# Summing modulation vectors over partition blocks on VectorE instead of TensorE, and writing gates as rows when they are computed

## The chip, the cores and the metric

The kernel runs on one core of one Trainium2 chip. The metric is the device time of one execution in microseconds. A core has TensorE (PE in the profile; the loads of its stationary operand are PEld), VectorE (DVE), ScalarE (ACT), GpSimd (POOL) and SyncE (SP), which works through its instructions in order and here issues most loads. ScalarE issues a few DMAs as well.

## The reference

Two layers of a diffusion backbone over 512 latent tokens of width 1024, with 256 context tokens. Each layer is a half-step SwiGLU, a token mixer (windowed attention in layer 0, a Fourier mix in layer 1), and a second half-step SwiGLU. Every sublayer is modulated by vectors that come from a conditioning vector:

```
mod = (silu(c) @ mod_w[i] + mod_b[i]).reshape(-1, 9, 1024)
h   = x * (1 + mod[:, 3j+1]) + mod[:, 3j]                        # shift and scale, sublayer j
y   = 0.5 * (a * silu(g)) @ wo        with a, g = split(h @ wi)  # the half-step SwiGLU
x   = layer_norm(alpha * x + mod[:, 3j+2] * y, g, b)             # gate
```

For layer 0 the vectors are also needed for the context stream, with its own conditioning vector c_ctx. All is float32.

## The kernel before, in words

**Stages.** One after the other: a head that computes the first shift and scale and the first seven weight blocks' products (h0), the rest of the latent half-step FFN of layer 0, the context half-step FFN, attention, then the FFN l1 (second of layer 0), the FFN l2 (first of layer 1), the Fourier mix, and the FFN l3 (second of layer 1). In an FFN the up products (tiles `up`) run over 22 pairs of weight blocks, and the down products (tiles `y`) over 22 blocks of 128 rows.

**Products in three parts.** Every float32 operand is split in a high and a low part (`wh` by ScalarE, `wl` by VectorE, line 177), and a product is three matmuls (line 181). `weights` (line 211) emits the split of a weight three blocks ahead of its use (`SPLIT_AHEAD`), and its load further ahead. A weight block of the down products may first be multiplied by a gate's row (`gate_next`, line 203: `wr<-wr,gr`), so that the gate costs nothing later.

**Modulation.** A vector of 1024 values needs all of a [1024, 1024] matrix. VectorE sums it: `mod_steps` (line 257) works through jobs, each 128 rows of mod_w, and adds row times silu(c) into an accumulator of [128, 1024], `acc`; eight jobs make a vector. Jobs of the vectors 2, 3 and 4 of layer 0 feed two accumulators (latent and context stream), the others one. The jobs are spread over the pairs of up products: 40 in the first FFN, 24 in the context FFN, 40 in l1, 40 in l2, none in l3. The sum over the 128 partitions then follows: `mod_fold` (line 233) transposes blocks of 32x32 on VectorE (`mt`) and reduces them to `mr` [128, 32], which leaves four partial sums in four blocks of 32 partitions. Three jobs later (`MOD_LAG`), `mod_reduce` (line 245) has TensorE add the four blocks with a matrix of ones at the right places (`folder`) into a PSUM bank `mp`, and VectorE adds the bias `mod_b` and writes the vector as columns [128, 8] into `mod`, in four instructions of 32x8.

**Gates.** A gate is needed as a row repeated on all partitions. `gate_row` (line 315), called in `late` (line 686) two pairs before the end of the up products, has ScalarE scale the columns (`gs`), write them to DRAM (`there`, 1024 elements of 4 bytes out of place), and load them back as a row for each partition (`gr`); both DMAs are issued by ScalarE, and the second waits for the first.

**Order.** TensorE's and GpSimd's instructions stay in program order. VectorE's and ScalarE's do so only in marked stretches (`pin`); in the FFNs, where the modulation runs, their order is set by a scheduler at build time from its own estimates. Tiles of [128, 1024] share 42 buffers (`slot`), small ones 20 (`small`). PSUM has two rings of four banks; a pair of up products takes one of each, `mp` took the next in turn.

Of the kernel before, what the change touches and what calls it, by code (L numbers as in the profile page):

```python
# [10 lines left out]
F32 = mybir.dt.float32  # L11
F32R = mybir.dt.float32r
AF = mybir.ActivationFunctionType
ALU = mybir.AluOpType

P = 128
D = 1024
KC = D // P
# [32 lines left out]
P_WIDTH = 648  # L51
CORE_FETCH = 6
CORE_TILES = 5
MOD_LAG = 3
MOD_EARLY = 1
TURN_ACT = 4
BETWEEN = 5
Q_TURN = 3
# [53 lines left out]
class Emitter:  # L112
# [34 lines left out]
    def small(self, shape, nm="sm"):  # L147
        return self.pool.tile(shape, F32, tag="small", name=self.name(nm), bufs=20)

    def hbuf(self, shape, nm):  # L150
        return self.pool.tile(shape, F32R, tag="h", name=self.name(nm), bufs=2)

# [72 lines left out]
    def mod_plan(self, jobs):  # L225
        self.jobs = [(l, v, streams, k) for (l, v, streams) in jobs for k in range(KC)]
        self.mraw = {}
        self.n_mraw = 0
        self.n_job = 0
        self.acc = {}  # L230
        self.due = []

    def mod_fold(self, l, v, s, a):


        nc = self.nc
        turned = self.slot([P, 1024], F32, "mt")
        nc.vector.transpose(turned, a)
        t = self.small([P, D // BLK], "mr")
        nc.vector.tensor_reduce(  # L240
            out=t, in_=turned.rearrange("p (c k) -> p c k", k=BLK), axis=mybir.AxisListType.X, op=ALU.add
        )
        return l, v, s, t

    def mod_reduce(self, l, v, s, t):
        nc = self.nc
        ps = self.bank(nm="mp")
        self.mm(ps[:, : D // BLK], self.folder, t, start=True, stop=True)
        per = P // BLK
        for q in range(per):  # L250
            rows = slice(q * BLK, (q + 1) * BLK)
            cols = slice(v * KC, (v + 1) * KC)
            nc.vector.tensor_tensor(
                self.mod[l][s][rows, cols], ps[rows, q : D // BLK : per], self.mod_b[l][rows, cols], ALU.add
            )

    def mod_steps(self, n, ahead=2):
        nc = self.nc
        for _ in range(n):
            if self.n_job >= len(self.jobs):  # L260
                break
            while self.n_mraw < min(self.n_job + ahead + 1, len(self.jobs)):
                l, v, _, k = self.jobs[self.n_mraw]
                r = self.slot([P, 1024], F32, "mr")
                nc.sync.dma_start(r, self.ins["mod_w"][l, v, k])
                self.mraw[self.n_mraw] = r
                self.n_mraw += 1
            l, v, streams, k = self.jobs[self.n_job]
            r = self.mraw.pop(self.n_job)
            self.n_job += 1  # L270
            while self.due and self.due[0][0] <= self.n_job:
                self.mod_reduce(*self.due.pop(0)[1])
            for s in streams:
                sc = self.silu_c[:, s, k : k + 1]
                if k == 0:
                    a = self.slot([P, 1024], F32, "acc")
                    self.acc[s] = a
                    nc.vector.tensor_scalar(a, r, sc, None, ALU.mult)
                else:
                    a = self.acc[s]  # L280
                    nc.vector.scalar_tensor_tensor(a, r, sc, a, ALU.mult, ALU.add)
                if k == KC - 1:
                    self.due.append((self.n_job + MOD_LAG, self.mod_fold(l, v, s, self.acc.pop(s))))

    def mod_finish(self, upto):
        if upto > self.n_job:
            self.mod_steps(upto - self.n_job)
        while self.due:
            self.mod_reduce(*self.due.pop(0)[1])

    def col(self, l, s, v):
        return self.mod[l][s][:, v * KC : (v + 1) * KC]
# [19 lines left out]
        return G, B  # L312


    def gate_row(self, l, s, j, scale):

        act = self.nc.scalar
        cols = self.small([P, KC], "gs")
        act.activation(cols, self.col(l, s, 3 * j + 2), AF.Copy, scale=scale)
        there = self.dram.tile([KC, P], F32, tag="gate", name=self.name("there"), bufs=2)  # L320
        act.dma_start(there.rearrange("c p -> p c"), cols)
        row = self.slot([P, 1024], F32, "gr")
        act.dma_start(row, there.rearrange("c p -> (c p)").unsqueeze(0).broadcast_to([P, D]))
        return row

    def fold(self, row, w0, n):
# [353 lines left out]
    def half_step(self, ups, down, h, x, N, l, s, j, nxt, quota, first=None, halves=False, held=None, mid=None, out_h=None, keep=True, fold=True, more=None, reach=REACH):  # L680

        us = []
        stat = self.halves_of(us, N)
        st = {}

        def late():
            self.mod_finish(self.n_job)
            gate = self.gate_row(l, s, j, 0.5)
            if fold:
                self.fold(gate, down, NF)  # L690
            else:
                st["gate"] = gate
            if more is not None:
                self.fold(self.gate_row(*more[0], 1.0), more[1], KC)
            stat(0)

        if N == CTX:
            mid = self.ffn_up_rows(ups, h, quota, us, first, late)
        else:
            self.ffn_up(ups, h, N, quota, us, first=first, halves=halves, late=late, held=held)  # L700
        st["x"] = x() if callable(x) else x

        st["ln"] = (l, j)

        def middle():
            if mid is not None:
                mid()
            if keep and nxt is None:
                st["rows"] = self.ln_rows(l, j)

        st["affine"] = None if nxt is None else self.affine_ln(l, j, nxt[0], s, nxt[1])
        if nxt is not None:
            st["h"] = out_h() if out_h is not None else self.new_h("h")
        rest = self.project(down, NF, stat, st, N // P, mid=middle, keep=keep, reach=reach)
        return rest, st


    def head(self):
# [11 lines left out]
        def load(k):  # L730
            raws[k] = []
            for i in range(2):
                r = self.slot([P, 4, 256], F32, "m0")
                sync.dma_start(r, ins["mod_head"][k, i])
                raws[k].append(r)
            if k == 0:
                sync.dma_start(self.mod_b[0], ins["mod_b"][0])
            if k % 2 == 0:
                xts[k // 2] = self.slot([P, 2, SEQ], F32, "xt")
            if k < 2:  # L740
                sync.dma_start(xts[0][:, k], ins["xT"][0][:, k])
            elif k % 2 == 0:
                sync.dma_start(xts[k // 2], ins["xT"][k // 2])
            ws[k] = self.slot([P, HEAD * P], F32, "wr")
            cuts = (0, HEAD_CUT, HEAD * P) if k == 0 else (0, HEAD * P)
            for c0, c1 in zip(cuts, cuts[1:]):
                sync.dma_start(ws[k][:, c0:c1], ins["wi_head"][k][:, c0:c1])
# [106 lines left out]
        load(1)  # L854
        load(2)
        gather(0, 0, KC)
        nc.vector.tensor_copy(bias[:, 0], self.mod_b[0][:, :KC])
        nc.vector.tensor_scalar(bias[:, 1], self.mod_b[0][:, KC : 2 * KC], 1.0, None, ALU.add)
        w_parts(0)
        for _ in whole_chunks(0):  # L860
            pass
# [30 lines left out]
    def constants(self):  # L892
# [3 lines left out]
        nc.vector.memset(self.ones, 1.0)  # L896
        self.mhalf = self.const([P, 16], F32, "mhalf")
        nc.vector.memset(self.mhalf, -0.5)
        self.mod_b, self.mod = [], []
        for l in range(DEPTH):  # L900
            self.mod_b.append(self.const([P, 9 * KC], F32, f"mod_b{l}"))
            self.mod.append([self.const([P, 9 * KC], F32, f"mod{l}_{s}") for s in range(2 if l == 0 else 1)])


# [1 line left out]
    def run(self):  # L906
# [43 lines left out]

        h, held = self.head()
        sync.dma_start(self.ident, ins["ident"])
        sync.dma_start(self.mod_b[1], ins["mod_b"][1])
        self.folder = self.const([P, P], F32, "folder")
        sync.dma_start(self.folder, ins["folder"])
        self.ln_g = self.const([P, 6 * KC], F32, "ln_g")
        self.ln_b = self.const([P, 6 * KC], F32, "ln_b")
        sync.dma_start(self.ln_g, ins["ln_g_col"])
# [53 lines left out]
            w_c0[0], w_c0[1], ch, load_cx, CTX, 0, 1, 0, (0, 1), 3 * KC, first=rest, out_h=ctx_h, keep=False, fold=False  # L1012
        )

        self.fold(self.gate_row(0, 0, 1, 1.0), w_ao, KC)
        stat = self.attention(w_kv, w_q, w_ao, h1, st["h"], rest)
        st = dict(x=x)
        st["affine"] = self.affine_ln(0, 1, 0, 0, 2)
# [48 lines left out]
    def attention(self, w_kv, w_q, w_ao, h1, ch, rest):  # L1067
# [135 lines left out]
        q10 = q_post(1, 0, ps)  # L1203
        mask = self.slot([P, 896], F32, "mask")
        sync.dma_start(mask, ins["mask"])
        nsink = self.const([P, HEADS], F32, "nsink")
        nc.vector.tensor_scalar(nsink, self.sink, -1.0, None, ALU.mult)


        oT = []  # L1210
# [282 lines left out]
def _constants():  # L1493
# [38 lines left out]
    for i, tab in enumerate(dft(SEQ)):  # L1532
# [1 line left out]
    t2 = t2.reshape(2, 2, 2, P, 512).transpose(0, 1, 3, 2, 4)  # L1534
    return {
        "ident": np.eye(P, dtype=np.float32),
        "folder": np.tile(np.eye(BLK, dtype=np.float32), (P // BLK, P // BLK)),
        "mask": mask,
        "rope": rope,
        "dft1": t1.reshape(P, 1024).astype(np.float32),  # L1540
# [4 lines left out]
def _layout(inp):  # L1545
    f = {k: np.asarray(v) for k, v in inp.items()}

    def cols(a):
        n = a.shape[0]
        return a.reshape(n, -1, P).transpose(0, 2, 1)  # L1550
# [9 lines left out]
    m["mod_w"] = f["mod_w"].reshape(DEPTH, KC, P, 9, D).transpose(0, 3, 1, 2, 4)  # L1560
    head = m["mod_w"][0, :2].reshape(2, KC, P, KC, P)
    m["mod_head"] = head.transpose(3, 2, 1, 0, 4).reshape(KC, P, 2, 4, 256).transpose(0, 2, 1, 3, 4)
    m["mod_b"] = cols(f["mod_b"])
    g = f["ln_g"].reshape(6, D)
    b = f["ln_b"].reshape(6, D)
    m["ln_g_col"] = g.reshape(6, KC, P).transpose(2, 0, 1).reshape(P, 6 * KC)
# [39 lines left out]
```

## Time and profile before

| | us |
|---|---|
| the runs shown | 1977.49, 1979.6, 1979.67 |
| their median | 1979.6 |
| the profiled execution | 1976.75 |
| its span | 1974.9 |

The span runs from the first to the last instruction in the trace; the execution's own time is 1.85 us more. The granted TensorE clock was 0.999 of full speed. Times within the trace are counted from the span's start. The names on both sides of `<-` are the program's tiles, written and read; `x` with a number counts instructions. L79 stands for nearly all instructions, since all go through one helper, so groups are told apart by their tiles. A matmul's duration reaches from its start to the end of its passage, and the next starts before that, so the pitch of matmuls is read from their starts.

### The profile page before, as it was taken

Reading aid. Unit: us, or ns where it says so; the run is one execution under the profiler, and the core shown is the slowest. Engines: PE = TensorE matmul, PEld = TensorE weight load, DVE = VectorE, ACT = ScalarE, POOL = GpSimd, SP = SyncE. Lnnn points to the kernel's source line nnn. Section 1 sums busy time; section 2 is a strip of 40 time slices with the busy share of each in tenths; the row PEclk is TensorE's granted clock in tenths of the full one; section 3 lists DMA queues with packets and bytes.
Section 4 is the critical chain, followed back from the end, with each engine's and each line's share of the span. In section 5 each row is a group of like instructions: output and inputs, shape, how many; then the busy total and the mean of one; then the engine's idle time right before and its main releaser. Section 6 shows DMA issues by size and latency. Waiting matters only on the chain.

```text
span 1974.9 us, 24216 instructions
## 1 busy us (share of the span) xinstructions
PE 1966.4 (100%) x9564; PEld 1643.7 (83%) x9564; DVE 1278.7 (65%) x1719; ACT 684.5 (35%) x991; POOL 72.6 (4%) x138
## 2 busy tenths in 40 slices
PE   9999999999999999999999999999999999999998
PEld 7888888888888888888888888888888988888887
DVE  8669985698656765666558456655766873333744
ACT  3322233443623784422224232222333642222420
POOL 0000000000000460000000000000000000000000
PEclk9999999999999999999999999999999999999999
DMA  9856633488722013555543335563441343222411
GB/s 358 298 192 210 206 119 126 148 310 254 278 81 74 13 43 107 192 189 197 195 134 126 110 124 210 188 202 129 149 129 63 118 112 102 85 96 86 140 63 43
DMA packets 90483, 296.21 MB, mean 150 GB/s; under 512 B 17281, under 2 KB 17665, under 8 KB 90369
## 3 DMA queue, kind: packets, MB, share of 16 engines
q1 hardware_dynamic: 82080, 290.96, 43.1%
q10 hardware_dynamic: 8288, 3.70, 0.7%
q8 instruction: 75, 1.23, 0.3%
q14 instruction: 40, 0.32, 0.1%
HBM read 292.50 MB, written 2.13 MB: 149 GB/s over the span
## 4 chain that ended last, share of the span: by engine, by line
PE 99%; DVE 0%; issue 0%; ACT 0%; DVEq 0%
PE up L79 55%; PE y L79 32%; PE qkv L79 4%; PE s L79 2%; PE o L79 2%; PE pt L79 2%; PE tp L79 1%; PE ab L79 1%; PE f L79 1%; PE qt L79 0%; PE ut L79 0%; PE ms L79 0%; PE rr L79 0%; PE mp L79 0%; PE kt L79 0%; DVE x L79 0%
## 5 line engine op out<-in xcount | busy, mean ns | idle before, releaser
L79 DVE TENSOR_TENSOR wl<-wr,wh 128x1024 fp32r<-128x1024 f32 (+1 forms) x367 | 429.3, 1193 | 102.8 <-ACT wh L79 68.6
L79 ACT CAST wh<-wr 128x1024 fp32r<-128x1024 f32 (+1 forms) x363 | 366.0, 1046 | 208.2 <-PE y L79 90.7
L79 PE MATMUL up<-hh,wh 128*128 128x512 f32 (+1 forms) x1128 | 425.1, 377 | 0.0
L79 PE MATMUL up<-hl,wh 128*128 128x512 f32 (+1 forms) x1128 | 423.7, 376 | 0.0
L79 PE MATMUL up<-hh,wl 128*128 128x512 f32 (+1 forms) x1128 | 423.6, 376 | 0.0
L79 PE MATMUL y<-wh,uh 128*128 128x512 f32 x924 | 303.3, 389 | 0.0
L79 PE MATMUL y<-wh,ul 128*128 128x512 f32 x924 | 302.3, 388 | 0.0
L79 PE MATMUL y<-wl,uh 128*128 128x512 f32 x924 | 302.2, 388 | 0.0
L79 ACT ACTIVATE sg<-up 128x512 f32<-128x512 f32 (+1 forms) x100 | 59.2, 594 | 657.9 <-PE up L79 657.8
L79 DVE TENSOR_TENSOR u<-up,sg 128x512 f32<-128x512 f32 x88 | 60.6, 690 | 327.2 <-PE up L79 319.3
L79 PEld LDWEIGHTS up<-hl,wh 128*128 128x128 f32 x1128 | 212.3, 188 | 38.5
L79 PEld LDWEIGHTS up<-hh,wl 128*128 128x128 f32 x1128 | 212.4, 188 | 38.1
L79 PEld LDWEIGHTS up<-hh,wh 128*128 128x128 f32 x1128 | 212.3, 188 | 38.0
L79 PEld LDWEIGHTS y<-wh,ul 128*128 128x128 f32 x924 | 173.5, 188 | 35.9
L79 PEld LDWEIGHTS y<-wl,uh 128*128 128x128 f32 x924 | 173.5, 188 | 35.4
L79 PEld LDWEIGHTS y<-wh,uh 128*128 128x128 f32 x924 | 173.3, 188 | 35.5 <-issue 0.4
L79 DVE SCALAR_TENSOR_TENSOR acc<-mr,silu_c,acc 128x1024 f32<-128x1024 f32 x147 | 186.1, 1280 | 1.3
L79 DVE TENSOR_TENSOR wr<-wr,gr 128x1024 f32<-128x1024 f32 x99 | 118.8, 1221 | 38.3 <-DMA wr<-in_wo_dram 20.6
L79 PE MATMUL up<-h0h,wl 128*128 128x512 f32 x352 | 131.0, 391 | 0.0
L79 PE MATMUL up<-h0h,wh 128*128 128x512 f32 x352 | 130.7, 394 | 0.1
L79 PE MATMUL up<-h0l,wh 128*128 128x512 f32 x352 | 130.3, 391 | 0.0
L79 DVE SCALAR_TENSOR_TENSOR x<-x,y 128x512 f32<-128x512 f32 x48 | 32.7, 682 | 99.3 <-PE y L79 99.1
(183 smaller groups left out, 2036.4 us busy)
## 6 DMA issues: line engine op xcount, KB each, us to landing
wr<-in_wi_dram SPq DMA_DIRECT2D x169, 512.0 KB, 4.5
mr<-in_mod_w_dram SPq DMA_DIRECT2D x144, 512.0 KB, 4.4
wr<-in_wo_dram SPq DMA_DIRECT2D x110, 512.0 KB, 4.2
wr<-in_wi_rows_dram SPq DMA_DIRECT2D x44, 512.0 KB, 4.8
m<-in_mod_head_dram SPq DMA_DIRECT2D x16, 512.0 KB, 9.9
wr<-in_wqkv_dram SPq DMA_DIRECT2D x12, 512.0 KB, 4.2
wr<-in_attn_wo_dram SPq DMA_DIRECT2D x8, 512.0 KB, 3.5
wr<-in_fourier_wo_dram SPq DMA_DIRECT2D x8, 512.0 KB, 3.6
```

The source lines that it names most:

```text
L79: ins = f(*args, **kw)
```

## The change

The matmul into `mp`, its constant `folder` and the lag are gone. `mod_fold` now does the rest on VectorE: three of the four blocks of `mr` and the bias are copied side by side into a tile of [32, 4, 32] (`mq`), reduced to [32, 32], and the first block is added. For shifts and scales, four copies write the columns into `mod`. For gates, VectorE transposes [32, 32], so that the vector lies in order as 32 rows of 32 values, halves it where the sublayer is a half step, and three jobs later ScalarE's queue writes it to a place in DRAM of its own. `gate_row` only loads it. The biases are laid out anew: the first two vectors' as columns for the head (128x16 instead of 128x72), and all in one constant of 128x160, in place of the second layer's 128x72. The attention sink's negation is written in place.

```diff
     def mod_fold(self, l, v, s, a):
-        nc.vector.transpose(turned, a)
+        vec.transpose(turned, a)
         t = self.small([P, D // BLK], "mr")
-        nc.vector.tensor_reduce(
+        vec.tensor_reduce(
             out=t, in_=turned.rearrange("p (c k) -> p c k", k=BLK), axis=mybir.AxisListType.X, op=ALU.add
         )
-        return l, v, s, t
-
-    def mod_reduce(self, l, v, s, t):
-        nc = self.nc
-        ps = self.bank(nm="mp")
-        self.mm(ps[:, : D // BLK], self.folder, t, start=True, stop=True)
         per = P // BLK
+        parts = self.fours([BLK, per, D // BLK], "mq")
+        n = l * 9 + v
+        vec.tensor_copy(parts[:, 0], self.mod_b4[n % per * BLK : (n % per + 1) * BLK, n // per])
+        for q in range(1, per):
+            vec.tensor_copy(parts[:, q], t[q * BLK : (q + 1) * BLK])
+        total = self.small([BLK, D // BLK], "ms")
+        vec.tensor_reduce(out=total, in_=parts.rearrange("p q c -> p c q"), axis=mybir.AxisListType.X, op=ALU.add)
+        vec.tensor_tensor(total, total, t[:BLK], ALU.add)
+        if v % 3 == 2:
+            row = self.small([D // BLK, BLK], "gr")
+            vec.transpose(row, total)
+            if v != 5:
+                vec.tensor_scalar(row, row, 0.5, None, ALU.mult)
+            self.gates[l, s, v // 3] = there = self.dram.tile(
+                [D // BLK, BLK], F32, tag=f"gate{l}{s}{v}", name=self.name("there"), bufs=1
+            )
+            self.due.append((self.n_job + GATE_LAG, there, row))
+            return
         for q in range(per):
-            rows = slice(q * BLK, (q + 1) * BLK)
-            cols = slice(v * KC, (v + 1) * KC)
-            nc.vector.tensor_tensor(
-                self.mod[l][s][rows, cols], ps[rows, q : D // BLK : per], self.mod_b[l][rows, cols], ALU.add
+            vec.tensor_copy(
+                self.mod[l][s][q * BLK : (q + 1) * BLK, v * KC : (v + 1) * KC], total[:, q : D // BLK : per]
             )
...
+    def gate_out(self):
+        _, there, row = self.due.pop(0)
+        self.nc.scalar.dma_start(there, row)
...
-    def gate_row(self, l, s, j, scale):
-        act = self.nc.scalar
-        cols = self.small([P, KC], "gs")
-        act.activation(cols, self.col(l, s, 3 * j + 2), AF.Copy, scale=scale)
-        there = self.dram.tile([KC, P], F32, tag="gate", name=self.name("there"), bufs=2)
-        act.dma_start(there.rearrange("c p -> p c"), cols)
+    def gate_row(self, l, s, j):
         row = self.slot([P, 1024], F32, "gr")
-        act.dma_start(row, there.rearrange("c p -> (c p)").unsqueeze(0).broadcast_to([P, D]))
+        there = self.gates[l, s, j]
+        self.nc.scalar.dma_start(row, there.rearrange("c i -> (c i)").unsqueeze(0).broadcast_to([P, D]))
         return row
...
-                sync.dma_start(self.mod_b[0], ins["mod_b"][0])
+                sync.dma_start(self.mod_b, ins["mod_b"])
...
-        sync.dma_start(self.mod_b[1], ins["mod_b"][1])
-        self.folder = self.const([P, P], F32, "folder")
-        sync.dma_start(self.folder, ins["folder"])
+        sync.dma_start(self.mod_b4, ins["mod_b4"])
```

`mod_steps` and `mod_finish` call `gate_out` where they called `mod_reduce`, and `mod_fold` at once where they put it in line.

More of the change, by code (lines that the diff above doesn't have):

```diff
@@ L53 @@
 CORE_TILES = 5
-MOD_LAG = 3
 MOD_EARLY = 1
+GATE_LAG = 3
 TURN_ACT = 4
@@ L148, in small, with fours @@
         return self.pool.tile(shape, F32, tag="small", name=self.name(nm), bufs=20)
+    def fours(self, shape, nm):
+        return self.pool.tile(shape, F32, tag="fours", name=self.name(nm), bufs=1)
     def hbuf(self, shape, nm):
@@ L231, in mod_plan @@
         self.due = []
+        self.gates = {}
     def mod_fold(self, l, v, s, a):
-        nc = self.nc
+        vec = self.nc.vector
         turned = self.slot([P, 1024], F32, "mt")
-        nc.vector.transpose(turned, a)
+        vec.transpose(turned, a)
         t = self.small([P, D // BLK], "mr")
-        nc.vector.tensor_reduce(
+        vec.tensor_reduce(
             out=t, in_=turned.rearrange("p (c k) -> p c k", k=BLK), axis=mybir.AxisListType.X, op=ALU.add
         )
-        return l, v, s, t
-    def mod_reduce(self, l, v, s, t):
-        nc = self.nc
-        ps = self.bank(nm="mp")
-        self.mm(ps[:, : D // BLK], self.folder, t, start=True, stop=True)
-        per = P // BLK
+        per = P // BLK
+        parts = self.fours([BLK, per, D // BLK], "mq")
[16 more added lines that the diff above has]
+            return
         for q in range(per):
-            rows = slice(q * BLK, (q + 1) * BLK)
-            cols = slice(v * KC, (v + 1) * KC)
-            nc.vector.tensor_tensor(
-                self.mod[l][s][rows, cols], ps[rows, q : D // BLK : per], self.mod_b[l][rows, cols], ALU.add
+            vec.tensor_copy(
+                self.mod[l][s][q * BLK : (q + 1) * BLK, v * KC : (v + 1) * KC], total[:, q : D // BLK : per]
             )
@@ L271, in mod_steps @@
             while self.due and self.due[0][0] <= self.n_job:
-                self.mod_reduce(*self.due.pop(0)[1])
+                self.gate_out()
             for s in streams:
@@ L282, in mod_steps @@
                 if k == KC - 1:
-                    self.due.append((self.n_job + MOD_LAG, self.mod_fold(l, v, s, self.acc.pop(s))))
+                    self.mod_fold(l, v, s, self.acc.pop(s))
     def mod_finish(self, upto):
@@ L288, in mod_finish @@
         while self.due:
-            self.mod_reduce(*self.due.pop(0)[1])
+            self.gate_out()
+    def gate_out(self):
+        _, there, row = self.due.pop(0)
+        self.nc.scalar.dma_start(there, row)
     def col(self, l, s, v):
@@ L687, in late @@
             self.mod_finish(self.n_job)
-            gate = self.gate_row(l, s, j, 0.5)
+            gate = self.gate_row(l, s, j)
             if fold:
@@ L693, in late @@
             if more is not None:
-                self.fold(self.gate_row(*more[0], 1.0), more[1], KC)
+                self.fold(self.gate_row(*more[0]), more[1], KC)
             stat(0)
@@ L856, in head @@
         gather(0, 0, KC)
-        nc.vector.tensor_copy(bias[:, 0], self.mod_b[0][:, :KC])
-        nc.vector.tensor_scalar(bias[:, 1], self.mod_b[0][:, KC : 2 * KC], 1.0, None, ALU.add)
+        nc.vector.tensor_copy(bias[:, 0], self.mod_b[:, :KC])
+        nc.vector.tensor_scalar(bias[:, 1], self.mod_b[:, KC:], 1.0, None, ALU.add)
         w_parts(0)
@@ L898, in constants @@
         nc.vector.memset(self.mhalf, -0.5)
-        self.mod_b, self.mod = [], []
+        self.mod_b = self.const([P, 2 * KC], F32, "mod_b")
+        self.mod_b4 = self.const([P, 5, D // BLK], F32, "mod_b4")
+        self.mod = []
         for l in range(DEPTH):
-            self.mod_b.append(self.const([P, 9 * KC], F32, f"mod_b{l}"))
             self.mod.append([self.const([P, 9 * KC], F32, f"mod{l}_{s}") for s in range(2 if l == 0 else 1)])
@@ L1013, in run @@
         )
-        self.fold(self.gate_row(0, 0, 1, 1.0), w_ao, KC)
+        self.fold(self.gate_row(0, 0, 1), w_ao, KC)
         stat = self.attention(w_kv, w_q, w_ao, h1, st["h"], rest)
@@ L1205, in attention @@
         sync.dma_start(mask, ins["mask"])
-        nsink = self.const([P, HEADS], F32, "nsink")
-        nc.vector.tensor_scalar(nsink, self.sink, -1.0, None, ALU.mult)
+        nsink = self.sink
+        nc.vector.tensor_scalar(nsink, nsink, -1.0, None, ALU.mult)
         oT = []
@@ L1536, in _constants @@
         "ident": np.eye(P, dtype=np.float32),
-        "folder": np.tile(np.eye(BLK, dtype=np.float32), (P // BLK, P // BLK)),
         "mask": mask,
@@ L1562, in _layout @@
     m["mod_head"] = head.transpose(3, 2, 1, 0, 4).reshape(KC, P, 2, 4, 256).transpose(0, 2, 1, 3, 4)
-    m["mod_b"] = cols(f["mod_b"])
+    m["mod_b"] = cols(f["mod_b"])[0, :, : 2 * KC]
+    rows = np.zeros((5, P // BLK, D), np.float32)
+    rows.reshape(-1, D)[: DEPTH * 9] = f["mod_b"].reshape(DEPTH * 9, D)
+    m["mod_b4"] = rows.reshape(5, P // BLK, D // BLK, BLK).transpose(1, 3, 0, 2).reshape(P, 5, D // BLK)
     g = f["ln_g"].reshape(6, D)
```

## The prediction

> **What bounds the kernel now.** I read the page first: the busy time of each engine, the VectorE row of the forty slices, and the chain that ended last.
>
> ```profile
> span 1974.9 us, 24216 instructions
> ...
> PE 1966.4 (100%) x9564; PEld 1643.7 (83%) x9564; DVE 1278.7 (65%) x1719; ACT 684.5 (35%) x991; POOL 72.6 (4%) x138
> ...
> DVE  8669985698656765666558456655766873333744
> ...
> PE 99%; DVE 0%; issue 0%; ACT 0%; DVEq 0%
> ```
>
> TensorE (PE) is busy all the time and is 99% of the chain. An edit is therefore worth what it takes out of TensorE's stream, or what it opens as a hole in it; VectorE (DVE) and ScalarE time counts only where it becomes such a hole. The place to watch is where VectorE's digits stand at 9. The profiled execution took 1976.75 us, 1.85 us more than its span of 1974.9. The runs shown lie at 1977.49, 1979.6 and 1979.67; the median, 1979.6, is 2.85 us above the profiled execution. I make the sum against 1976.75 and add 2.85 at the end.
>
> **What the removed matmuls cost.** The change takes out every matmul into mp. This is the table of the five stretches of up products, for the instructions that write or read mp alone:
>
> ```profile
> 47.59:257.08 209.49, 2.18 (x16) 2.54 (x16) 5.16 (x32) 1.00 0.64 221
> 379.46:505.44 125.98, 0.90 (x6) 1.13 (x6) 1.93 (x12) 1.00 0.84 284
> 810.02:1047.41 237.39, 1.51 (x10) 1.88 (x10) 3.19 (x20) 1.00 0.52 179
> 1174.98:1412.36 237.38, 1.51 (x10) 1.88 (x10) 3.19 (x20) 1.00 0.52 177
> 1611.71:1847.72 236.01, 0.00 (x0) 0.00 (x0) 0.00 (x0) 1.00 0.31 98
> ```
>
> The first number after the stretch is its length, then come mp's busy time on PE, its weight loads, and VectorE's additions behind it. One mp matmul leaves two PE records (16 records are 8 matmuls): 8, 3, 5, 5 and 0, together 21. The last three stretches run the same 22 pairs of products with the same shapes; two of them hold five mp matmuls, the last none. The difference is 237.39 - 236.01 = 1.38 us and 237.38 - 236.01 = 1.37 us, so 0.275 us for one mp. This is measured inside one execution and holds all that an mp does to its neighbours.
>
> In the first stretch mp matmuls come singly or, where one pass over mod_w feeds both streams, in twos. The chain in order of time shows it; its columns are start, length, what:
>
> ```profile
> 135.65 0.14 PE mp L79 x2
> 135.79 32.77 PE up L79 x144
> 168.56 0.36 PE mp L79 x4
> 168.93 32.77 PE up L79 x144
> 201.70 0.36 PE mp L79 x4
> 202.06 32.77 PE up L79 x144
> 234.83 0.36 PE mp L79 x4
> 235.19 21.89 PE up L79 x96
> ...
> 1047.41 108.80 PE y L79 x480
> ```
>
> Without mp a 512-wide product comes every 108.80/480 = 0.2267 us, 144 of them in 32.64 us. From 168.93 to 202.06 is 33.13 us: a pair of mp costs 0.49. The first stretch has two single ones and three pairs: 2 x 0.275 + 3 x 0.49 = 2.02 us. The context stretch has 3 x 0.275 = 0.82, the two long ones 1.38 + 1.37 = 2.75. Together **5.6 us** leave TensorE's stream.
>
> The Trainium skill, "TensorE: Matmul & The Clock Gate", section "LDWEIGHTS (loading the stationary operand)", prices a weight load by its columns over 1.2 per ns: 107 ns for 128 columns, so an estimate of 213 ns for the two loads of an mp and 4.5 us for 21. The measured difference of the two stretches, 0.275 us, is larger and decides.
>
> **What is added on VectorE.** Until now a vector costs VectorE a transpose, a reduction and four additions of 32x8. Now four copies of 32x32 follow the reduction, then a reduction of 32x(32 times 4), an addition of 32x32, and then four copies of 32x8 (14 vectors) or a 32x32 transpose and, but for the mixer's gates, a multiplication (7 gates). No row shows a 32x32 instruction. The nearest, from the groups by shape:
>
> ```profile
> L79 DVE TENSOR_REDUCE mr<-mt 128x32 f32<-128x1024 f32 x21 | 25.1, 1207 | 0.3
> ...
> L79 DVE TENSOR_TENSOR mod<-mp,mod_b 32x8 f32<-32x8 f32 x84 | 13.5, 160 | 1.7 <-PE mp L79 0.7
> ...
> L79 DVE TENSOR_TENSOR ra<-kvb,rope 128x128 f32<-128x128 f32 x8 | 1.9, 284 | 0.0
> ```
>
> 8 elements take 160 ns and 128 take 284, about 1.03 ns per element over a fixed part, so 32 take 186 ns; I use 0.19 us. The reduction over 128 elements follows the slope from 1024 elements at 1207 ns and comes to 0.29. The timeline tells how closely they follow each other:
>
> ```profile
> 206.13 1.38 DVE L79 TENSOR_TENSOR mod<-mp,mod_b 32x8 f32<-32x8 f32 x8
> ...
> 745.55 0.16 DVE L79 TENSOR_SCALAR s<-mod 128x8 f32<-128x8 f32 x1
> 745.74 0.17 DVE L79 TENSOR_TENSOR G<-ln_g,s 128x8 f32<-128x8 f32 x1
> 745.83 0.16 DVE L79 TENSOR_TENSOR B<-ln_b,s 128x8 f32<-128x8 f32 x1
> ```
>
> Eight additions that move from one block of 32 partitions to the next take 1.38 us, 0.17 each: they do not overlap. An instruction that needs the one before starts 0.03 after its end (745.55 + 0.16 to 745.74). One that doesn't, on the same partitions, starts 0.08 before it (745.74 + 0.17 to 745.83). So a plain vector costs 4 x 0.19 + 0.32 + 0.22 + 4 x 0.17 = 1.98 us and a gate 0.76 + 0.32 + 0.22 + 0.22 + 0.20 = 1.72, where the four additions cost 0.69: VectorE grows by 14 x 1.29 + 7 x 1.03 = 25 us to about 1304. The lower bound takes 0.16 us for each new instruction and an overlap of 0.08, the upper 0.284 for each of 32 elements.
>
> The Trainium skill, "VectorE: DVE Perf Modes", section "Two Vector instructions with no wait between them", says that an instruction whose input or output starts in another quadrant of partitions than the last is held until all before it are done; the eight additions in 1.38 us agree. Its section "Rules for kernel authors" asks to minimize the number of chained instructions, which speaks against this change. If the new copies were not held, they would follow 0.08 us earlier each and the hole priced next would close: 5.6 us by that, 5.0 with holding.
>
> Where does this reach TensorE? Here are two of the stretches again, with all instructions (length, then PE, weight loads and, third, VectorE), and VectorE alone in three windows of 144 products each, in which two streams are summed:
>
> ```profile
> 379.46:505.44 125.98, 125.98 (x584) 104.75 (x583) 109.59 (x126) 59.61 (x79) 0.55 (x1) 1.00 0.84 284
> 810.02:1047.41 237.39, 237.39 (x1104) 198.79 (x1103) 146.04 (x161) 59.58 (x76) 0.00 (x0) 1.00 0.52 179
> ```
>
> ```profile
> 135.79:168.93 33.14, 33.03 (x35) 1.00 0.62 206
> 168.93:202.06 33.13, 31.86 (x37) 1.00 0.60 212
> 202.06:235.19 33.13, 32.66 (x38) 1.00 0.51 138
> ```
>
> With one stream VectorE has 91 us and 16 us to spare, and 1.3 us more per vector disappear in them. With two it has nearly none. The timeline at the end of the third window:
>
> ```profile
> 232.27 2.35 DVE L79 TENSOR_TENSOR wl<-wr,wh 128x1024 fp32r<-128x1024 f32 x2
> 234.94 0.69 DVE L79 TENSOR_TENSOR u<-up,sg 128x512 f32<-128x512 f32 x1 [0.31 <-ACT uh L79]
> ...
> 238.12 1.22 DVE L79 TENSOR_TENSOR wl<-wr,wh 128x1024 fp32r<-128x1024 f32 x1
> 239.41 2.36 DVE L79 TENSOR_TENSOR wr<-wr,gr 128x1024 f32<-128x1024 f32 x2
> ```
>
> VectorE is idle for 0.11, 1.27 and 0.47 us, 0.31 of the last only after the two weight splits at 232.27: 1.5 us before them. Up to there two gates and four plain vectors now add 2 x 1.72 + 4 x 1.98 = 11.4 us, while 20 old additions (3.5 us) fall away: 7.9 more work, 1.5 taken by idle time, so the splits at 232.27 come 6.4 us later. When are they needed? One more split (238.12) follows before gated down weights begin (239.41), so they are the third and second to last weights of the up products, each used by 24 matmuls; the y products begin at 235.19 + 21.89 = 257.08, so the first is used at 257.08 - 3 x 24 x 0.2267 = 240.8 us. The first ends at 233.5: 7.3 us of cover. TensorE itself comes 2.0 earlier, so 5.3 remain against 6.4: **a hole of 1.1 us**. If the order on VectorE, which isn't written out by hand here, puts the splits ahead of the last two vectors' small instructions (4 us), there is none. I take 0.6.
>
> **The rest at nothing.** Gates are now written as 32 rows of 128 bytes when computed, where late() had to gather 4-byte elements and wait:
>
> ```profile
> ACT uh L79 <- DMA there<-gs: 12.7, 2, 9.1
> ...
> DVE wr L79 <- DMA gr<-there: 10.0, 2, 9.0
> ACT ident_r L79 <- DMA there<-gs: 9.4, 1, 9.4
> ```
>
> These waits (total, times, longest, in us) go, with no gain: TensorE didn't stop behind them. The new write waits, in ScalarE's queue, for VectorE's row; the casts of weights (wh) are queued behind it, and VectorE's splits wait for those. But it is issued three jobs after the chain, so the row is there; if not, the cover at the tightest place is the 5.3 us worked out above. In SP's queue one small load falls away after the head, and mod_b in the head shrinks from 36 to 8 KB:
>
> ```profile
> m<-in_mod_head_dram SPq DMA_DIRECT2D x16, 512.0 KB, 9.9
> ```
>
> At that pace 28 KB are worth 0 to 0.5 us; a loss is excluded, since no load there grows. I take 0, because loads of 512 KB on both sides set what arrives when. Raw loads that wait for buffers which VectorE frees shift by its lateness, and are issued two weights (48 x 0.2267 = 10.9 us) ahead. PSUM banks only come freer. Sum: -5.6 + 0.6 = **-5.0 us**: 1971.75 for the profiled execution, 1974.6 as median.
>
> **Rivals.** First, VectorE overruns by more: with 0.284 us for each 32-element instruction (5 per plain vector, 7 per gate) the two-stream stages add 0.094 x (4 x 5 + 2 x 7) = 3.2 us, the hole grows to 4.3, and 1.3 us are left: 1978.3, no change that can be seen. For it: VectorE at 96 to 100% there. Against: the slope of the rows gives 0.19.
>
> Second, slower: the same hole, but each small instruction that shifts partitions or walks with a stride takes about twice what the rows suggest. The 56 small instructions of the two-stream stages must cost 0.15 us more each, 0.34 instead of 0.19, before the hole passes 5.6 + 4 us; then 1983.6 or more. Against: no row of a small instruction is that long.
>
> Third, the saving isn't there because the neighbours of an mp are slow for another reason, and only its own chain pieces vanish (0.14 us for a single one, 0.36 for a pair: 15 x 0.14 + 3 x 0.36 = 3.2 us): with the hole 2.6 less, 1977.0. Against: the stretch without mp is shorter by the whole 1.37.
>
> **How the numbers follow.** A difference under 0.2% (4 us) is about what a measurement of this kernel can't tell from none; the runs shown spread over 2.2 us. The forecast has a chance of 0.72, the first rival 0.14, the second 0.06, the third 0.08. Of the forecast's 0.72, holes of 0 to 1.6 us and the spread put 0.04 inside 0.2%; so faster 0.68, same 0.26, slower 0.06. The range runs from 5.6 us off the fastest of the executions (1971.1) to the first rival with a run at the top of the spread: 1979.5.
>
> **What would show it.** The changed profile should have no mp, the two long stretches at 236.0 us like the last, VectorE near 1304 us, and, in the first stretch, the third to last up weight used right behind its split, near 239 us, with at most some 1.6 us of idle time there. The forecast is wrong if the long stretches keep 237.4 us, or if holes elsewhere add up to more than 2 us: behind ScalarE's new writes, in the head, or at the start of the context stage.

## The result, and the profile after: slower, with fewer instructions on TensorE

The changed kernel takes **1995.57 us** (median of four runs, 1995.3 to 1996.8); the kernel before, in four runs beside them, 1978.62 (1977.49 to 1979.67). The ratio is 1.0087, with an interval of 1.0069 to 1.0104: 17 us slower. The prediction said 1974.6 us and faster; its range ended at 1979.5. One run in this document, one of the ten of experiment 3, took 2175.73 us at a granted clock of 0.85; the ratio there leaves it out.

The profiled execution of the changed kernel took 1995.3 us. Its page, the same lines as were shown of before:

```profile
span 1993.3 us, 24199 instructions
...
PE 1984.2 (100%) x9522; PEld 1641.4 (82%) x9522; DVE 1298.9 (65%) x1829; ACT 682.7 (34%) x984; POOL 72.5 (4%) x138
...
DVE  8679985698656765766558456655866862333744
...
PE 99%; DMA 0%; DVE 0%; SPq 0%; issue 0%; ACT 0%; DVEq 0%
```

TensorE has 42 instructions fewer, two for each of the 21 matmuls into `mp`, and is busy for 17.8 us longer. It is still 99% of the chain, so it does not wait more. The engine's list of waits says the same (total, times, longest, in us); these two, both in the head, are all that it names on PE:

```profile
PE up L79 <- DVE mhalf L79: 0.9, 1, 0.9
PE ms L79 <- DMA m<-in_mod_head_dram: 0.3, 1, 0.3
```

So the same products take longer. Where? The five stretches of up products again (the length is followed by PE, weight loads, VectorE, ScalarE and GpSimd, then by TensorE's granted clock, the DMA share and GB/s):

```profile
48.44:261.05 212.61, 212.61 (x915) 172.24 (x916) 172.85 (x233) 55.18 (x67) 0.00 (x0) 1.00 0.62 214
383.44:508.50 125.06, 125.06 (x578) 104.07 (x577) 112.09 (x141) 59.33 (x78) 0.55 (x1) 1.00 0.84 299
814.13:1055.75 241.62, 241.62 (x1093) 198.35 (x1093) 150.87 (x187) 59.53 (x75) 0.00 (x0) 1.00 0.51 176
1183.28:1424.90 241.62, 241.62 (x1094) 198.36 (x1093) 150.52 (x185) 58.30 (x74) 0.00 (x0) 1.00 0.51 174
1624.26:1865.87 241.61, 241.61 (x1093) 198.37 (x1093) 85.57 (x87) 58.10 (x74) 0.00 (x0) 1.00 0.29 96
```

The last row is the one to read. That stretch, l3, holds no `mp` before, and after it holds nothing of the change but the load of one gate's row near its end; VectorE works for a third of it, loads are few, the clock is 1.00. It took 236.01 us and takes 241.61. The chain in order of time (start, length, what) shows what did not change:

```profile
1055.75 108.85 PE y L79 x480
...
1624.26 241.62 PE up L79 x1092
```

480 down products take 108.85 us, where they took 108.80. The up products have become slower and the down products have not, in a stage that the change does not touch. Only the context stretch, whose operands are not the latent h, behaves as forecast: 125.98 to 125.06.

The timeline of TensorE in that stretch (start, length) gives the pitch, from one start to the next:

```profile
1699.79 0.39 PE L79 MATMUL up<-hh,wh 128*128 128x512 f32 x1
1700.02 0.39 PE L79 MATMUL up<-hh,wl 128*128 128x512 f32 x1
1700.25 0.40 PE L79 MATMUL up<-hl,wh 128*128 128x512 f32 x1
...
1701.65 0.39 PE L79 MATMUL up<-hl,wh 128*128 128x512 f32 x1
```

Eight pitches from 1699.79 to 1701.65 are 1.86 us, 0.2325 each, spread evenly over the three parts. It is no stall somewhere but 5.7 ns on every product of 512 columns. A stretch of 1092 such pieces holds 984 that are 512 wide and 108 that are 256 wide, and by their starts the narrow ones keep their pitch of 0.120 us: 5.6 us over 984 are 5.7 ns.

The accounting: the three long stretches have gained 4.23, 4.24 and 5.60 us, the first one 3.12, what precedes it 0.85 (it starts at 48.44 instead of 47.59), and the context stretch has lost 0.92. That is 17.1 of the 18.4 us between the two spans; most of the other 1.3 lies in attention, where the products into `qkv` read h as well.

**Theories.** One: the place of the operands in SBUF. All constants that exist when the 42 shared buffers are allocated lie ahead of them. The built program's addresses show that the resizing (2176 bytes per partition instead of 2048) moved the shared buffers from 51616 to 51744, while the buffers of h stayed at 16800 and 33184. From h to a shared buffer it was a multiple of 256 bytes (34816 = 136 x 256), and now it is 128 more. An up product has one operand in each (h moving, a weight stationary), a down product has both in shared buffers, a multiple of 4096 bytes apart. So the pitch would depend on the distance between the two operands, modulo some power of two. Two, the rival: the new instructions on VectorE, or the new DMAs, disturb TensorE's reads. The even 5.7 ns in l3, where no vector is summed, already speaks against it. Three: it is the absolute address of a shared buffer that counts, or the order in which the scheduler placed things.

### The profile page after: what moved, and what is told of

Read it like the earlier page. It is cut to its first block, busy times and chain, and to the rows that moved or that the text cites. A ratio compares the mean times of both kernels' runs of the same rounds, so it can differ in the third digit from the quotient of the medians.

```text
span 1993.3 us, 24199 instructions
## 1 busy us (share of the span) xinstructions
PE 1984.2 (100%) x9522; PEld 1641.4 (82%) x9522; DVE 1298.9 (65%) x1829; ACT 682.7 (34%) x984; POOL 72.5 (4%) x138
## 4 chain that ended last, share of the span: by engine, by line
PE 99%; DMA 0%; DVE 0%; SPq 0%; issue 0%; ACT 0%; DVEq 0%
PE up L79 55%; PE y L79 31%; PE qkv L79 4%; PE s L79 2%; PE o L79 2%; PE pt L79 2%; PE tp L79 1%; PE f L79 1%; PE ab L79 1%; DMA m<-in_mod_head_dram 0%; PE qt L79 0%; PE ut L79 0%; PE rr L79 0%; SPq L79 0%; PE ms L79 0%; PE kt L79 0%
## 5 line engine op out<-in xcount | busy, mean ns | idle before, releaser
L79 PE MATMUL up<-hh,wh 128*128 128x512 f32 (+1 forms) x1128 | 429.6, 381 | 0.0
L79 PE MATMUL up<-hl,wh 128*128 128x512 f32 (+1 forms) x1128 | 429.1, 380 | 0.0
L79 PE MATMUL up<-hh,wl 128*128 128x512 f32 (+1 forms) x1128 | 429.1, 380 | 0.0
```

What stands on the lines that cost most here:

```text
L79: ins = f(*args, **kw)
```

## Experiments

**1. The change with the old distance.** Two constants of 192 bytes each, which were allocated after the shared buffers, are allocated ahead of them. 128 + 384 = 512 bytes, so the distance is a multiple of 256 again. Nothing else differs.

```diff
         nc.vector.memset(self.mhalf, -0.5)
+        self.ln_g = self.const([P, 6 * KC], F32, "ln_g")
+        self.ln_b = self.const([P, 6 * KC], F32, "ln_b")
         self.mod_b = self.const([P, 2 * KC], F32, "mod_b")
...
-        self.ln_g = self.const([P, 6 * KC], F32, "ln_g")
-        self.ln_b = self.const([P, 6 * KC], F32, "ln_b")
```

> The changed kernel, with the two layer-norm constants (384 bytes per partition) allocated ahead of the 42 shared buffers instead of behind them, so that these lie 0 bytes off the h tiles modulo 512, as before the change, where the change had put them at 128. Address theory (the pitch of the products with h depends on how the shared buffers lie to h): the last stretch of up products goes from 241.5 back to 236.0 us, all stretches have pitch 0.2267, and the kernel takes about 1973 us (1978.6 less 5.6 for the mp matmuls). Rival (the pitch comes from the change's own work, VectorE's small instructions or the other use of PSUM banks): 1995.6 us as the changed kernel, the last stretch at 241.5.

Measured: 1971.63 us (seven runs, 1971.27 to 1972.91) against 1976.97 for the kernel before on the same chip; ratio 0.9972, interval 0.9961 to 0.9983. The change is faster by 5.3 us when the buffers lie as they did. Its chain:

```profile
47.55 207.47 PE up L79 x914
255.02 108.80 PE y L79 x480
...
807.10 236.01 PE up L79 x1092
...
1605.91 236.01 PE up L79 x1092
```

The long stretches (l2 as well) stand at 236.01 and the first is at 207.47. The same place in the timeline:

```profile
1699.64 0.39 PE L79 MATMUL up<-hh,wh 128*128 128x512 f32 x1
1699.87 0.39 PE L79 MATMUL up<-hh,wl 128*128 128x512 f32 x1
...
1701.45 0.39 PE L79 MATMUL up<-hl,wh 128*128 128x512 f32 x1
```

Eight pitches in 1.81 us, 0.226 each. From the changed kernel's span of 1993.3 to 1969.3 are 24.0 us, nearly all of them for the moved buffers (experiment 8 adds them up); from 1974.9 to 1969.3 are the 5.6 us that the rest of the change saves. This version is faster than the kernel before and than the changed one.

**2. The kernel before with 128 bytes more.** The rival needs the change's instructions. Here there are none: two constants of 64 bytes are allocated earlier.

```diff
         nc.vector.memset(self.mhalf, -0.5)
+        self.nsink = self.const([P, HEADS], F32, "nsink")
+        self.sink = self.const([P, HEADS], F32, "sink")
...
-        self.sink = self.const([P, HEADS], F32, "sink")
...
-        nsink = self.const([P, HEADS], F32, "nsink")
+        nsink = self.nsink
```

> The kernel before, with nothing changed but that the sink and its negation (128 bytes) are allocated ahead of the shared buffers, so that these lie where the changed kernel has them, 128 bytes off h modulo 512. Address theory: all up products with h and the qkv products get the pitch 0.2323 instead of 0.2267, the three long stretches 5.5 us longer each, the first 4.6 to 5.1, attention about 1 to 2, the head 0.4: 1978.6 + 23 to 24 = about 2002 us. Rival: 1978.6, no change.

Measured: 1999.27 us (four runs), 22.3 above the kernel before beside it; ratio 1.011, interval 1.0095 to 1.0125. The loss is there without the change, and the stretches of up products are as long as in the changed kernel:

```profile
1060.27 108.85 PE y L79 x480
...
1629.92 241.62 PE up L79 x1092
```

The second theory falls.

**3 and 4. The kernel before with 256 and 384 bytes more.** These ask for the period: `ln_g` and `sink` early (256), and `ln_g` and `ln_b` early (384).

```diff
+        self.ln_g = self.const([P, 6 * KC], F32, "ln_g")
+        self.sink = self.const([P, HEADS], F32, "sink")
```

```diff
+        self.ln_g = self.const([P, 6 * KC], F32, "ln_g")
+        self.ln_b = self.const([P, 6 * KC], F32, "ln_b")
```

> The kernel before with the shared buffers 256 bytes off h modulo 512 (256 bytes of constants allocated ahead). Address theory, if a multiple of 256 (or less) is enough: 1978.6. If only 512 will do: slower, by 23 us or another amount. A pitch under 0.2267, and so under 1978, is possible too, if 0 isn't the best distance. Rival: 1978.6.

> The kernel before with the shared buffers 384 bytes off h modulo 512 (384 bytes of constants allocated ahead). Address theory: as at 128 if the distance counts by its size either way (about 2002), or another pitch; unchanged only if the rule is about something else. Rival: 1978.6.

Measured: with 256 bytes 1977.5 us, ratio 1.000 (0.999 to 1.0009); with 384 bytes 2000.43 us, ratio 1.0117 (1.01 to 1.0134). The l3 stretch of the first:

```profile
1613.27 236.01 PE up L79 x1092
```

and of the second:

```profile
1629.61 241.62 PE up L79 x1092
```

It isn't "any shift" and isn't the order of allocation: 256 is as good as 0, and 384 as bad as 128.

**5 and 6. The kernel before with 64 and 32 bytes more.** One run each (`sink` early; `mhalf` with 24 columns instead of 16).

```diff
+        self.sink = self.const([P, HEADS], F32, "sink")
```

```diff
-        self.mhalf = self.const([P, 16], F32, "mhalf")
+        self.mhalf = self.const([P, 24], F32, "mhalf")
```

> The kernel before with the shared buffers 64 bytes off h modulo 256 (the sink's 64 bytes allocated ahead). What the runs so far showed (pitch 0.2268 at 0 and 256, 0.2324 at 128 and 384) leaves open what smaller distances do. If the pitch depends only on whether the distance is a multiple of 256: 0.2324 and about 1999 us. If it grows with the distance up to 128: about 0.2296 and 1988. If 64 is harmless: 1977.

> The kernel before with the shared buffers 32 bytes off h modulo 256 (one constant 32 bytes longer). A multiple of 256 needed: 0.2324 and about 1999 us. A growth with distance: about 0.228 and 1982. A distance better than 0 would show as a pitch under 0.2267.

Measured: 2000.37 and 2003.41 us, beside 1977.07 for the kernel before. The chain with 64 bytes, first products of attention and l3:

```profile
573.60 11.01 PE qkv L79 x48
...
1629.44 241.99 PE up L79 x1092
```

and with 32 bytes:

```profile
573.61 11.20 PE qkv L79 x48
...
1632.11 242.38 PE up L79 x1092
```

None of the smaller steps tried (32, 64 and 128) is free for the up products. With 64 bytes the products into `qkv` lose less (11.01/48 = 0.2294 us) than with 32 (0.2333), though up products lose about the same in both. In `qkv` the roles are changed: h is the stationary operand and the weight moves. Experiment 8 takes that up.

**7. The distance or the address?** The changed kernel, with its shared buffers where the change put them (51744), but with h moved up by the same 128 bytes: `mhalf` and `mod_b` are allocated ahead of h.

```diff
+        self.mhalf = self.const([P, 16], F32, "mhalf")
+        self.mod_b = self.const([P, 2 * KC], F32, "mod_b")
         h = self.new_h("h0")
...
-        self.mhalf = self.const([P, 16], F32, "mhalf")
...
-        self.mod_b = self.const([P, 2 * KC], F32, "mod_b")
```

> The changed kernel, its shared buffers at the very addresses of the change, but with 128 bytes of constants allocated ahead of the h tiles, so that h moves too and the distance is 0 again. If the distance between the two operands counts: pitch 0.2268, last long stretch 236.0, about 1971.6 us. If the absolute address of the shared buffers counts: 0.2324 and 1995.5.

Measured in one run: 1971.42 us, the time of experiment 1. The chain:

```profile
47.76 207.47 PE up L79 x914
...
1606.15 236.01 PE up L79 x1092
```

The absolute address of the shared buffers is not what counts. Nor is it the order of the instructions: in the traces of experiments 1 and 7, VectorE's 1829 and ScalarE's 984 instructions come in the same order, by tile, as in the changed kernel's. The third theory falls, and the distance is left.

**8. The distance by itself.** A kernel that computes nothing of the reference: TensorE multiplies one tile of rounded float32 by another, 48 matmuls for each distance from the stationary to the moving operand, 512 columns wide and then 256, while the other engines stand still. Its total time means nothing.

```
for i in range(COUNT):
    w = weights[:, i % 8 * P : (i % 8 + 1) * P]
    at = d // 4 + i % 3 // 2 * step
    tc.keep_in_program_order(
        nc.tensor.matmul(o[:, :n], w, moving[:, at : at + n], start=(i == 0), stop=(i == COUNT - 1))
    )
```

`w` is stationary and steps by 512 bytes; `at` counts elements of 4 bytes, and `step` is 1024 of them.

> Not the model: only float32r matmuls of 128x128 by 128x512 (then 128x256) on TensorE, 48 for each of twenty distances between the moving operand and the stationary one (0 to 480 bytes in steps of 32 modulo 512, then 4, 16, 260 and 512), with no other engine at work in those stretches; the output is not the reference's. If the distance alone sets the pitch, inside TensorE: 0.2267 us at 0, 256 and 512, and 0.229 to 0.234 at all others; of the 256-wide ones no forecast. Rival (the slow pitch needs VectorE's or ScalarE's accesses to the same buffers at that moment): one pitch for all distances. The total time has no meaning here.

Its windows, one from the first start of a group to the first start of the next. In this order: 512 wide at a distance of 0, 32, 64, 128, 192, 256 and 4 bytes, then 256 wide at 0 and 32. The length over 48 is the pitch.

```profile
52.91:63.78 10.87, 10.87 (x49) 9.01 (x48) 0.00 (x0) 0.00 (x0) 0.00 (x0) 1.00 0.01 2
63.78:74.99 11.21, 11.21 (x50) 9.00 (x48) 0.00 (x0) 0.00 (x0) 0.00 (x0) 1.00 0.00 0
74.99:85.99 11.00, 11.00 (x50) 9.02 (x48) 0.00 (x0) 0.00 (x0) 0.00 (x0) 1.00 0.01 1
97.20:108.40 11.20, 11.20 (x50) 9.01 (x48) 0.00 (x0) 0.00 (x0) 0.00 (x0) 1.00 0.00 0
119.64:130.84 11.20, 11.20 (x50) 9.03 (x49) 0.00 (x0) 0.00 (x0) 0.00 (x0) 1.00 0.00 0
142.02:152.91 10.89, 10.89 (x50) 9.01 (x49) 0.00 (x0) 0.00 (x0) 0.00 (x0) 1.00 0.01 2
231.14:242.51 11.37, 11.37 (x50) 9.02 (x48) 0.00 (x0) 0.00 (x0) 0.00 (x0) 1.00 0.01 1
275.87:281.62 5.75, 5.75 (x49) 5.75 (x48) 0.00 (x0) 0.00 (x0) 0.00 (x0) 1.00 0.00 0
281.62:287.28 5.66, 5.66 (x50) 5.66 (x49) 0.00 (x0) 0.00 (x0) 0.00 (x0) 1.00 0.01 3
```

At 0 and 256 (and 512) bytes the pitch is 0.227 us, at 64 (and 320) 0.229, at the other multiples of 32 tried 0.233 to 0.234, at 4 bytes 0.237. It repeats after 256 bytes, needs no other engine, and has a direction: 64 is cheap and 192 is not. That explains experiment 5. A shared buffer 64 bytes further from h gives `qkv` (weight moving, h stationary) a distance of 64: 0.2294 there, 0.229 here. For up products (h moving) the same shift is -64, which is 192: their mean pitch over the trace of experiment 5 is 0.2333, and at 192 it is 0.2333 here.

The loss in the changed kernel, 5.7 ns a product, is a little under the 6.6 ns here at 128 bytes; why is open. Experiment 1 and the changed kernel differ by 16.8 us in the long stretches, 5.1 in the first, 0.9 ahead of it and 1.3 in `qkv`, together 24.1, against 24.0 us between their spans. Of the 0.9, some 0.7 is not the pitch: in the changed kernel the first block of 21 up products in the head starts at 21.23 us instead of 20.50, on a chain that comes through a load of the head. With 256 bytes (experiment 3), where the pitch is the good one, it starts at 21.04. So about 23.3 us are the moved buffers'.

**9. How much room VectorE had.** The prediction's own worry, lateness on VectorE, remained to be tested. Experiment 1's kernel, with the small instructions behind the sum of the first FFN's vectors 2, 3 and 4 made three times (the repeated ones write the same values).

```diff
-        vec.tensor_copy(parts[:, 0], self.mod_b4[n % per * BLK : (n % per + 1) * BLK, n // per])
-        for q in range(1, per):
-            vec.tensor_copy(parts[:, q], t[q * BLK : (q + 1) * BLK])
...
+        for _ in range(3 if l == 0 and v in (2, 3, 4) else 1):
+            vec.tensor_copy(parts[:, 0], self.mod_b4[n % per * BLK : (n % per + 1) * BLK, n // per])
+            for q in range(1, per):
+                vec.tensor_copy(parts[:, q], t[q * BLK : (q + 1) * BLK])
+            vec.tensor_reduce(out=total, in_=parts.rearrange("p q c -> p c q"), axis=mybir.AxisListType.X, op=ALU.add)
+            vec.tensor_tensor(total, total, t[:BLK], ALU.add)
...
-        for q in range(per):
+        for q in list(range(per)) * (3 if l == 0 and v in (3, 4) else 1):
```

> The changed kernel at distance 0, with VectorE's new small instructions done three times over for the six vectors of the two-stream stages (the result is the same). It tests the step of the prediction that VectorE's lateness reaches TensorE once the cover of the weight splits is used up. There are 5.0 us of cover at the tightest weight in the run at distance 0. Two more rounds cost 2 x 1.3 per gate and 2 x 1.95 per plain vector, 13 us before the last pair of vectors and 7.8 in it. Cover theory: TensorE gets holes of 7 to 15 us between 195 and 245 us in the first stretch, total about 1979 to 1987. Rival (the scheduler or the later slack hides it all): 1971.6.

Measured in one run: 1987.46 us, 15.8 more than experiment 1. TensorE's waits:

```profile
PE up L79 <- DVE wl L79: 5.7, 2, 4.9
PE y L79 <- DVE u L79: 5.0, 1, 5.0
```

The holes are real once VectorE is late enough: 5.7 us behind weight splits, the kind that the prediction priced. The other 5.0 are of a kind it had not seen, and come at 268 us, behind the stretch that was expected: the twentieth down product, the first into its PSUM bank, waits until VectorE's `u` has read that bank. The windows right behind the two long stops show what they cost beyond their own length (the granted clock is third from the end):

```profile
222.60:226.00 3.40, 3.38 (x8) 2.64 (x9) 3.31 (x10) 1.04 (x1) 0.00 (x0) 0.54 0.47 159
...
273.00:277.00 4.00, 3.93 (x9) 3.14 (x10) 3.96 (x10) 1.04 (x1) 0.00 (x0) 0.50 0.37 131
```

After each stop the granted clock is about half: 8 products in 3.40 us and 9 in 4.00, where 15 and 17.6 would fit, so 1.6 and 1.9 us more are lost. Holes and clock make 14.2 of the 15.8 us. The Trainium skill, "TensorE: Matmul & The Clock Gate", section "What's actually happening", says that TensorE runs at half rate after an idle window of about 3.4 us and until it has been busy for as long again; these rows agree.

## Why the prediction was wrong

**Step 1, the removed matmuls: right.** 5.6 us were to leave TensorE's stream. With the old distance the first stretch falls from 209.49 to 207.47 (2.02 forecast, 2.02 measured) and the long ones from 237.39 and 237.38 to 236.01; the context stretch falls from 125.98 to 125.16 (0.82 forecast, 0.82 measured). The spans differ by 5.6. The third rival, by which only the pieces of `mp` in the chain would vanish, is thereby out.

**Step 2, VectorE: right within 5 us.** About 1304 us were forecast, 1298.9 measured. The largest groups of new instructions in the changed kernel (busy time in us, then mean ns of one):

```profile
L79 DVE COPY mq<-mr 32x32 f32<-32x32 f32 x63 | 10.8, 171 | 1.1
L79 DVE COPY mod<-ms 32x8 f32<-32x8 f32 x56 | 9.0, 160 | 0.6
L79 DVE TENSOR_REDUCE ms<-mq 32x32 f32<-32x128 f32 x21 | 7.7, 367 | 0.0
L79 DVE TENSOR_TENSOR ms<-ms,mr 32x32 f32<-32x32 f32 x21 | 3.7, 175 | 0.2
```

The 32x32 copies and additions take 171 and 175 ns where 190 were used (the slope of the prediction's two rows gives 185, not 186), the reduction 367 where 290 were. With the copies of the bias (3.5 us), the transposes (1.4) and the multiplications (0.8) all groups come to 36.9 us; 13.5 fall away, so 23.4 more; other groups took 3.2 less. The first rival needed 0.284 us for each and the second 0.34; of the new instructions only the reduction, one for each vector, was that long.

**Step 3, the hole of 1.1 us, taken as 0.6: none came.** The branch named there, that the scheduler puts the splits ahead of the last vectors' small instructions, is what happened. VectorE's timeline in experiment 1:

```profile
232.58 1.20 DVE L79 TENSOR_TENSOR wl<-wr,wh 128x1024 fp32r<-128x1024 f32 x1
233.81 0.54 DVE L79 COPY mq<-mr 32x32 f32<-32x32 f32 x3
234.38 1.23 DVE L79 TENSOR_TENSOR wl<-wr,wh 128x1024 fp32r<-128x1024 f32 x1
```

The split that was to come 6.4 us late comes at 232.58 instead of 232.27. Its weight is used at 238.77 (near 239 was forecast), 5.0 us after the split's end. The mistake in the step was to count all six vectors' small instructions ahead of it; only four reductions into `ms` lie there. At the step's own prices these four vectors would still have left 2.4 us of lateness (7.4 - 3.5 - 1.5), and 0.3 was measured. In the kernel before, both of the last two reductions into `mr` (1.2 us each) came ahead of the splits, and now one comes behind them; how the rest divides among the prices isn't worked out. That this cover decides once it is used up is shown by experiment 9.

**Step 4, "The rest at nothing": this one failed.** It went through the gates (the wait of `wr` for `gr<-there` did fall, from 10.0 to 3.3 us, with no gain, as said), SP's load, PSUM and the loading of `mod_b`, and said of the last that a loss is excluded "since no load there grows". It priced the constants as traffic, not as sizes. Their sizes move every buffer that is allocated behind them, and that cost about 23.3 us in the profiled executions, four times what the change saves. No rival held it either: the one on the slower side was lateness of VectorE. Nor did "what would show it" ask for it: it spoke of long stretches that keep 237.4 us or of holes, and not of a stretch without `mp` that grows without a hole.

Could it have been read beforehand? Not the price: in the trace of before all products with an operand in h stand at the one distance, a multiple of 256. What could be seen was that the constants ahead of the shared buffers change their total by 128 bytes, and that every fixed pitch in the sum was measured with the old addresses. That would have been a reason for a wider range, upward as well as downward. (The range's upper end doesn't follow from its own terms either: 1978.3 with a run at the top of the spread, 0.07 above the median, is 1978.4 and not 1979.5.)

**What stays open.** Which part of TensorE makes the distance matter isn't shown, nor why 256 columns behave otherwise. The Trainium skill, "SBUF — State Buffer", section "Who interferes with whom", gives TensorE two independent read ports, one for the moving operand and one for weight loads, and says that it never waits on anyone. With no other engine at work the pitch here still depends on where the two operands lie to each other, 0.227 or 0.233 us; on that the measurement decides. Other types and other shapes were not tried.

## What to carry to other kernels

When TensorE bounds a kernel, the pitch of its products can depend on the addresses as well: an edit that resizes or reorders constants can change every product whose operands lie on both sides of them, so note where the large buffers land before and after. For products of 512 columns of rounded float32, as here, keep the distance between the two operands at a multiple of 256 bytes, padding if need be; for 256 columns 32 bytes were better than 0, so other shapes have to be measured. When a profile is slower without a new wait, compare a stage that the edit doesn't touch, by pitch, before looking at the stages that it does. And undo an edit's side effects one by one: here the change was worth 5.3 us of gain with the old distance and came out as 17 us of loss.

## What was not expected of the hardware

- TensorE's pitch for 512 columns of rounded float32 depends on the distance from the stationary to the moving operand modulo 256 bytes: 0.227 us at 0, 0.229 at 64, 0.233 to 0.234 at the other multiples of 32, 0.237 at 4, with no other engine at work. In the model it was 0.2324 at 128.
- For 256 columns the sign is the other way: 0.1198 us at 0 and 0.1179 at 32 bytes.
- Two stops of TensorE of 5 us each were followed by 3.4 to 4 us at half the clock, which added a third to their cost.
- On VectorE a reduction from 32x(32 by 4) to 32x32 takes 367 ns, twice an addition of 32x32 (175 ns).
